# Down projection of a hybrid decoder trunk: weight sums made by accumulating transfers, and eight pairs of k blocks with seven products in place of seven

## The chip, the cores and the metric

The kernel runs on one core of one Trainium2 chip. The metric is the time of one execution on the device in microseconds (us). The kernel before takes 2270.06 us, the median of three runs (2269.26 to 2272.61). The engines of a core work side by side, each through its own queue in order: TensorE (PE, matmuls into PSUM), VectorE (DVE), ScalarE (ACT), GpSimd (POOL) and SyncE (SP), which here only issues transfers.

## The reference

One layer of a decoder: two token mixers, a cross-attention and a feed-forward part, on 256 tokens of 2048 features, float32 throughout. The change touches the last product alone, the down projection of the feed-forward part:

```python
def conv_glu_ffn(u, w_up, conv_w, conv_b, w_down):
    gate, up = jnp.split(u @ w_up, 2, axis=-1)
    gate = causal_dwconv(gate, conv_w, conv_b)
    return (jax.nn.gelu(gate, approximate=False) * up) @ w_down

    # in reference(), for the one layer:
    u = rms_norm(h, ffn_norm_g[l])
    h = h + conv_glu_ffn(u, ffn_w_up[l], ffn_conv_w[l], ffn_conv_b[l], ffn_w_down[l])
    return rms_norm(h, final_norm_g)
```

w_down is 5632 x 2048. The result is added to h and normalised once more.

## The kernel before

**Weights as hi and lo.** Every float32 weight is split into two parts for PE: `hi`, the weight rounded to PE's format (an ACT copy), and `lo`, what is left (a DVE subtraction). The activations are split likewise. A product is then three matmuls, hi x hi, hi x lo and lo x hi (`mm_tok`, 512 columns each).

**The flow of weights.** Weights come in tiles of 128 x 2048 floats (1 MB) in one fixed order (`order`), into three buffers `raw`. `weights()` is called once for every tile that PE is about to use, and issues tiles up to two ahead of it (`AHEAD`): `issue()` starts the transfer on SP, then makes hi and lo in pieces of 1024 columns (L126, L127). hi and lo have five buffers each of 1024 columns (`WB`), which come free as PE has used them. So a `raw` buffer comes free when the tile three before it has been converted, and a conversion waits for its tile's transfer and for a buffer that PE gives back.

**The down projection.** It runs in two halves of 1024 output columns. A half is 22 steps, and a step takes one weight tile: two k blocks of 128 by two column blocks of 512. An ordinary step is 2 x 4 products, 24 matmuls, into four accumulators (2 token blocks x 2 column blocks). A step "with seven products" treats its 2 x 2 blocks in Strassen's way: seven products of sums of blocks in place of eight, 21 matmuls, into the four accumulators and four more (`own`) that collect what several results share. `down_steps` says which steps are of which kind; before, they are steps 2, 5, 8, 11, 14, 17 and 19 of a half, each on a pair q of k blocks, seven pairs in all. Such a step needs

- sums of the four weight blocks, called b11, b22, b12 and b21 (`seven_forms`): four additions on DVE (L164 to L169) in the `raw` tile, in between the conversions (L158, L159), since a sum overwrites a block already converted. It makes seven forms, 3 x 1024 + 512 columns of hi and lo, which take four of the five buffers;
- sums of the four activation blocks (`input_forms`): eight DVE and two ACT instructions for each pair, made once, during the first half (at j = 0, 3, 6, ...), through one buffer `c`, and kept in `xs` and in `ha` for the second half.

**What else stands around.** In each half, `gr` loads the final gain, and at j = 0, 4, 8, 12 `hr` loads two blocks of h, which eight matmuls with the identity add to the accumulators. After the last step with seven products the `own` accumulators are joined into `c` (L1016 to L1023). In the first half that begins with a critical section: ACT loads a function table and copies `own[0]`. The program is cut into blocks there (the UNCONDITIONAL_BRANCH rows below); ACT goes into the section only when everything that the engines and the transfer queues were given in the block before has been done. The other engines do not wait for it. At the very end, for each token block, four results are finished (L1026 add, L1028 square and sum, L1030 gain), a row sum gives the factor r (L1034, L266, L267), and the rows are scaled and stored (L1037 to L1043).

**What sets the order.** A scheduler places the instructions of each engine by its own estimate of when each is ready; the order that a kernel is written in is only its start.

Of the kernel before, what the change touches and what calls it, by code (L numbers as in the profile page):

```python
# [9 lines left out]
F32 = mybir.dt.float32  # L10
# [4 lines left out]
ALU = mybir.AluOpType  # L15
# [4 lines left out]
P = 128  # L20
# [23 lines left out]

NST = 7


def down_steps(half):  # L50
    rest = list(range(NST, KF // 2))
    if half:
        rest = rest[-4:] + rest[:-4]
    steps = []
    for s in range(NST):
        steps += [(False, rest.pop(0)) for _ in range(2 if s < NST - 1 else 1)] + [(True, s)]
    return steps + [(False, k) for k in rest]


# [5 lines left out]
def hybrid_trunk(ctx, tc, xT, memT, par, cst, msk, w_k0, w_ka, w_va, w_hg, w_hv, w_ghg, w_bhg, w_dt,  # L65
# [70 lines left out]
    def issue():  # L136
        seven = state["issued"] in sums
        src, w = fetch()
        cols = w[1]
        nc.sync.dma_start(out=w[0][:, 0:cols], in_=src)  # L140
        if seven:
            ready.append(seven_forms(w[0]))
            return
        half = (cols // 256) * 128
        halves(w, 0, half)
        halves(w, half, cols)
        ready.append(w[2])

    def seven_forms(raw):


        b11, b22, b12, b21 = [raw[:, 512 * i:512 * (i + 1)] for i in range(4)]
        forms = []

        def both(c, d):
            hi = wp.tile([P, 1024], F32R, name="hi", bufs=WB)
            lo = wp.tile([P, 1024], F32R, name="lo", bufs=WB)
            S.copy(out=hi[:, 0:d - c], in_=raw[:, c:d])  # L158
            V.tensor_tensor(out=lo[:, 0:d - c], in0=raw[:, c:d], in1=hi[:, 0:d - c].bitcast(F32),  # L159
                            op=ALU.subtract)  # L160
            forms.extend((hi[:, i:i + 512], lo[:, i:i + 512]) for i in range(0, d - c, 512))

        both(0, 1024)
        V.tensor_tensor(out=b11, in0=b11, in1=b12, op=ALU.add)  # L164
        V.tensor_tensor(out=b12, in0=b12, in1=b22, op=ALU.add)
        V.tensor_tensor(out=b22, in0=b11, in1=b22, op=ALU.add)  # L166
        both(0, 1024)
        both(1024, 2048)
        V.tensor_tensor(out=b21, in0=b22, in1=b21, op=ALU.add)  # L169
        both(1536, 2048)  # L170
        return forms

    background = []

# [750 lines left out]


    fd = ctx.enter_context(tc.tile_pool(name="fd", bufs=1))
    xs = big.tile([P, NST, 3, 256], F32R, name="s2")

    def inputs(k, g):  # L930
# [28 lines left out]
    for i in range(2):  # L959
# [8 lines left out]
        for j, (seven, q) in enumerate(steps):  # L968
            last = i == 1 and j >= len(steps) - 2
            if i == 0:  # L970
                for s in range(NST):
                    if j == 3 * s:
                        input_forms(s)
            w = weights()
            if last and j < len(steps) - 1:
                held = w, q
# [7 lines left out]
            elif seven:  # L984
# [85 lines left out]
def _layout(inp):  # L1070
# [19 lines left out]
    dn = np.stack([np.stack([dn[i, q][[0, 1, 0, 1], [0, 1, 1, 0]] if seven else  # L1090
                             dn[i, q].reshape(4, P, 512) for seven, q in down_steps(i)])
                   for i in range(2)])

# [63 lines left out]
```

## Time and profile before

| | |
|---|---|
| median of three runs | 2270.06 us |
| profiled execution | 2271.94 us, span 2269.6 us |
| PE, DVE, ACT busy | 99%, 71%, 59% |
| GpSimd busy | 1.3 us, nine instructions |
| transfers | 434.81 MB, mean 192 GB/s |
| down projection | about 2018.7 to 2260.4 us of the span on PE, then its tail to 2269.6 |

The view of stretches gives, for each stretch of the span, each engine's busy time with the number of instructions in it, the clock granted to PE, the share of the transfer engines that is busy and the GB/s. A row of the timeline is a start, a duration, an engine, a line, what is written and read, and in brackets the idle time just before it with what ended it. A row of the issues gives the size of a transfer and the time from issue to landing. Rows of groups give busy time, the mean of one in ns, and idle time before with what ended it.

### The profile page before, as it was taken

To read this page: it belongs to the slowest core of one execution; us is meant where nothing else is said; L and a number is where in the kernel's file an instruction comes from. 1 tells how busy PE (TensorE), PEld (TensorE's weight loads), DVE (VectorE), ACT (ScalarE), POOL (GpSimd) and SP (SyncE) were. 2 spreads that over 40 slices of the span, in tenths; PEclk is the share of its full clock that TensorE was granted. 3 is DMA by queue.
4 is the path that set the end of the run, shared out by engine and by line. 5 is a ranking of instruction groups with operands and counts; after the bars stand their busy time and mean duration, and the time that the engine had idled before them with its cause. 6 is when DMAs were issued, how large, how long until landed. Compare 5 with 4: busy or idle time off the path is not lost.

```text
span 2269.6 us, 33643 instructions
## 1 busy us (share of the span) xinstructions
PE 2255.6 (99%) x13368; PEld 1944.1 (86%) x13368; DVE 1622.6 (71%) x2622; ACT 1346.7 (59%) x2028; POOL 1.3 (0%) x9
## 2 busy tenths in 40 slices
PE   9999999999999999999999999999999999999998
PEld 8888888888888888888888888888888888888786
DVE  8878879796446677754576765667777777788776
ACT  7566767676446777854456645556555555555544
POOL 0000000000000000000000000000000000000000
PEclk9999999999999999999999999999999999999999
DMA  8644444546555555455566544565555555555563
GB/s 314 234 171 183 168 170 165 181 154 214 187 198 182 193 186 183 171 181 199 186 237 212 201 167 167 183 217 192 188 186 188 190 194 190 186 204 199 183 230 130
DMA packets 70044, 434.81 MB, mean 192 GB/s; under 512 B 7904, under 2 KB 12544, under 8 KB 20864
## 3 DMA queue, kind: packets, MB, share of 16 engines
q1 hardware_dynamic: 69456, 432.09, 53.7%
q8 instruction: 104, 1.70, 0.3%
q10 hardware_dynamic: 432, 0.58, 0.1%
q14 instruction: 52, 0.43, 0.1%
HBM read 426.32 MB, written 6.32 MB: 191 GB/s over the span
## 4 chain that ended last, share of the span: by engine, by line
PE 98%; DVE 1%; DMA 0%; ACT 0%; issue 0%; SPq 0%; DVEq 0%; ACTq 0%
PE proj L82 88%; PE misc L82 5%; PE lev L82 4%; DVE lo L127 0%; DMA hr<-h_d 0%; PE lev L750 0%; PE lev L686 0%; DMA raw<-in_w_k 0%; DVE e L505 0%; PE lev L830 0%; DVE e L518 0%; DVE lo L159 0%; ACT hi L126 0%; DVE h L1037 0%; DVE sm L564 0%
## 5 line engine op out<-in xcount | busy, mean ns | idle before, releaser
L127 DVE TENSOR_TENSOR lo<-raw,hi 128x1024 fp32r<-128x1024 f32 x738 | 888.5, 1221 | 386.5 <-ACT hi L126 252.5
L126 ACT CAST hi<-raw 128x1024 fp32r<-128x1024 f32 x738 | 771.4, 1049 | 528.3 <-PE proj L82 497.1
L82 PE MATMUL proj<-s,hi 128*128 128x512 f32 x3952 | 953.7, 393 | 0.3 <-ACT hi L343 0.3
L82 PEld LDWEIGHTS proj<-s,hi 128*128 128x128 f32 x3952 | 726.3, 188 | 143.8 <-issue 1.0
L82 PE MATMUL proj<-hi,s 128*128 128x512 f32 x1706 | 534.7, 390 | 0.0
L82 PEld LDWEIGHTS proj<-s,lo 128*128 128x128 f32 x3952 | 509.4, 191 | 20.6
L82 PE MATMUL proj<-s,lo 128*128 128x256 f32 x3952 | 515.9, 283 | 0.0
L82 PEld LDWEIGHTS proj<-hi,s 128*128 128x128 f32 x1706 | 320.1, 188 | 66.3 <-issue 0.3
L82 PE MATMUL proj<-lo,s 128*128 128x512 f32 x853 | 332.1, 389 | 0.0
L82 PEld LDWEIGHTS proj<-lo,s 128*128 128x128 f32 x853 | 160.1, 188 | 32.4
L247 ACT COPY jt<-proj 128x256 f32<-128x256 f32 x199 | 73.4, 369 | 101.5 <-PE proj L82 101.1
L158 ACT CAST hi<-raw 128x1024 fp32r<-128x1024 f32 (+1 forms) x56 | 51.6, 942 | 80.3 <-DVE raw L166 49.2
L909 DVE SCALAR_TENSOR_TENSOR gc<-g,par_t,gc 128x255 f32<-128x255 f32 x88 | 42.6, 484 | 55.1 <-ACT gc L907 53.6
L159 DVE TENSOR_TENSOR lo<-raw,hi 128x1024 fp32r<-128x1024 f32 (+1 forms) x56 | 60.0, 1089 | 26.3 <-ACT hi L158 25.8
L649 DVE SCALAR_TENSOR_TENSOR sz<-t,par_t,sz 128x255 f32<-128x255 f32 (+2 forms) x96 | 46.2, 481 | 20.5 <-ACT sz L646 19.2
L258 DVE SCALAR_TENSOR_TENSOR s<-h,par_t,s 128x256 fp32r<-128x256 f32 x32 | 15.4, 484 | 34.5 <-ACT s L257 34.5
L253 ACT COPY jt<-proj 128x256 f32<-128x256 f32 x32 | 11.8, 371 | 42.2 <-DVE h L252 42.2
L82 PE MATMUL proj<-hi,ha 128*128 128x512 f32 x104 | 36.3, 392 | 0.5 <-ACT hi L158 0.5
L518 DVE TENSOR_TENSOR e<-e,kq 128x256 f32<-128x256 f32 x96 | 34.2, 417 | 0.0
L505 DVE TENSOR_TENSOR e<-bb 128x256 f32<-128x256 f32 x96 | 33.6, 420 | 0.4
L82 PE MATMUL lev<-hi,s 128*128 128x512 f32 x92 | 32.7, 391 | 0.0
L509 ACT ACTIVATE e<-e 128x768 f32<-128x768 f32 x32 | 26.6, 842 | 3.5 <-DVE e L505 3.5
(288 smaller groups left out, 1717.4 us busy)
## 6 DMA issues: line engine op xcount, KB each, us to landing
raw<-in_w_up SPq DMA_DIRECT2D x88, 1024.0 KB, 4.8
raw<-in_w_hg SPq DMA_DIRECT2D x48, 1024.0 KB, 4.8
raw<-in_w_m SPq DMA_DIRECT2D x48, 1024.0 KB, 4.8
raw<-in_w_dn SPq DMA_DIRECT2D x44, 1024.0 KB, 4.8
raw<-in_w_hv SPq DMA_DIRECT2D x16, 1024.0 KB, 4.9
raw<-in_w_ghg SPq DMA_DIRECT2D x16, 1024.0 KB, 4.7
raw<-in_w_bhg SPq DMA_DIRECT2D x16, 1024.0 KB, 4.7
raw<-in_w_gm SPq DMA_DIRECT2D x16, 1024.0 KB, 4.8
```

The lines of the kernel that those rows point to most:

```text
L82: ins = PE.matmul(*args, **kwargs)
L126: S.copy(out=hi[:, c - a:d - a], in_=raw[:, c:d])
L127: V.tensor_tensor(out=lo[:, c - a:d - a], in0=raw[:, c:d], in1=hi[:, c - a:d - a].bitcast(F32), op=ALU.subtract)
L158: S.copy(out=hi[:, 0:d - c], in_=raw[:, c:d])
L159: V.tensor_tensor(out=lo[:, 0:d - c], in0=raw[:, c:d], in1=hi[:, 0:d - c].bitcast(F32), op=ALU.subtract)
L247: S.copy(out=tmp, in_=ps[:, T:2 * T])
L258: V.scalar_tensor_tensor(out=dst[:, T:2 * T], in0=src, scalar=g, in1=dst[:, 0:T].bitcast(F32), op0=ALU.mult, op1=ALU.subtract)
L505: V.tensor_tensor(out=lev[hw].rearrange("p (n c i) -> p n c i", c=2, i=hw), in0=free(bb, 0, [(2 * hw, nb), (T + hw, 2), (1, hw)]), in1=fre ...
L509: S.activation(out=e[j], in_=e[j], func=AF.Exp)
L518: V.tensor_tensor(out=ev, in0=ev, in1=free(kq, 0, [(2 * hw, nb), (T + hw, 2), (1, hw)]), op=ALU.mult)
L649: V.scalar_tensor_tensor(out=o[:, s:T], in0=raw[:, 0:T - s], scalar=pc("m2_cw", 4 * c + 3 - s), in1=o[:, s:T], op0=ALU.mult, op1=ALU.add)
L909: V.scalar_tensor_tensor(out=gc[:, s:T], in0=g[:, 0:T - s], scalar=pc("f_cw", 3 * c + 2 - s), in1=gc[:, s:T], op0=ALU.mult, op1=ALU.add)
```

## The change

Three things change.

*Two of the four weight sums are made by transfers.* The tile of a step with seven products now comes in parts. SP loads three blocks and a second copy of the first of them into `raw`, and b11 into a tile of its own (one buffer, `b11`). GpSimd then issues two transfers that add a block from memory to what lies in `raw`: these give the sums t1 and t3. DVE makes the other two (L173, L175 of the changed kernel). Conversions (L166, L167) are 512 + 3 x 1024 columns as before. Such a tile now moves 1.79 MB instead of 1.05 MB.

*Eight pairs instead of seven.* The steps with seven products are now 2, 5, 8, 10, 13, 15, 17 and 19 of a half. Input forms are made at every second step instead of every third, eight times.

*The seven products come in another order:* own[0], own[1], acc[1], acc[0], own[3], own[2], acc[2], which is the order in which the forms are now made.

```diff
-NST = 7
+NST = 8
...
-    for s in range(NST):
-        steps += [(False, rest.pop(0)) for _ in range(2 if s < NST - 1 else 1)] + [(True, s)]
+    for s, ordinary in enumerate((2, 2, 2, 1, 2, 1, 1, 1)):
+        steps += [(False, rest.pop(0)) for _ in range(ordinary)] + [(True, s)]
...
+        if seven:
+            ready.append(seven_forms(src, w[0]))
+            return
         nc.sync.dma_start(out=w[0][:, 0:cols], in_=src)
-        if seven:
-            ready.append(seven_forms(w[0]))
-            return
...
-        b11, b22, b12, b21 = [raw[:, 512 * i:512 * (i + 1)] for i in range(4)]
...
+        b11 = extra[0].tile([P, 512], F32, name="b11")
+        nc.sync.dma_start(out=raw[:, 0:1536], in_=src[:, 0:1536])
+        nc.sync.dma_start(out=raw[:, 1536:2048], in_=src[:, 0:512])
+        nc.sync.dma_start(out=b11, in_=src[:, 1536:2048])
+        G.dma_start(out=raw[:, 0:512], in_=src[:, 1536:2048], accum_op=ALU.add)
+        G.dma_start(out=raw[:, 1536:2048], in_=src[:, 512:1024], accum_op=ALU.add)
...
-        both(0, 1024)
-        V.tensor_tensor(out=b11, in0=b11, in1=b12, op=ALU.add)
-        V.tensor_tensor(out=b12, in0=b12, in1=b22, op=ALU.add)
-        V.tensor_tensor(out=b22, in0=b11, in1=b22, op=ALU.add)
-        both(0, 1024)
-        both(1024, 2048)
-        V.tensor_tensor(out=b21, in0=b22, in1=b21, op=ALU.add)
-        both(1536, 2048)
-        return forms
+        b11, = both(b11)
+        t1, b22 = both(raw[:, 0:1024])
+        V.tensor_tensor(out=raw[:, 512:1024], in0=raw[:, 0:512], in1=raw[:, 512:1024], op=ALU.add)
+        b21, t3 = both(raw[:, 1024:2048])
+        V.tensor_tensor(out=raw[:, 1024:1536], in0=raw[:, 512:1024], in1=raw[:, 1024:1536], op=ALU.add)
+        t2, t4 = both(raw[:, 512:1536])
+        return [b11, b22, t1, t2, t3, b21, t4]
...
-                for s in range(NST):
-                    if j == 3 * s:
-                        input_forms(s)
+                if j % 2 == 0 and j < 2 * NST:
+                    input_forms(j // 2)
...
                 mm_tok(own[0], a11, w[0], **one)
+                mm_tok(own[1], y1, w[2], **one)
                 mm_tok(acc[1], x4, w[1])
-                mm_tok(own[1], y1, w[2], **one)
+                mm_tok(acc[0], a12, w[5])
+                mm_tok(own[3], y3, w[4], **one)
                 mm_tok(own[2], x2, w[3], **one)
-                mm_tok(own[3], y3, w[4], **one)
-                mm_tok(acc[0], a12, w[5])
                 mm_tok(acc[2], a22, w[6])
```

`both` now makes the hi and lo of one part and returns them in pieces of 512 columns. `_layout` stores the blocks of such a tile in the order that these transfers read.

The scheduler places things anew. Three places matter below. In the rows, numbers behind a name tell buffers apart; a line number of the changed kernel is some six higher than that of the same line before.

ACT at the switch between the halves, before: raw_20033 is the tile of step 19, raw_20086 that of step 20, and lev_19308 is own[0].

```order
L158 CAST hi_20042<-raw_20033 128x1024
L158 CAST hi_20046<-raw_20033 128x1024
L1015 NO_OP
L1153 UNCONDITIONAL_BRANCH
L1016 ACT_TABLE_LOAD
L1017 COPY c_20151<-lev_19308 128x512
L1015 UNCONDITIONAL_BRANCH
L1015 NO_OP
L158 CAST hi_20051<-raw_20033 128x512
L126 CAST hi_20088<-raw_20086 128x1024
```

And now, where raw_20083, raw_20129 and raw_20163 are the tiles of steps 19, 20 and 21:

```order
L166 CAST hi_20099<-raw_20083 128x1024
L166 CAST hi_20104<-raw_20083 128x1024
L126 CAST hi_20131<-raw_20129 128x1024
L126 CAST hi_20135<-raw_20129 128x1024
L1021 NO_OP
L1159 UNCONDITIONAL_BRANCH
L1022 ACT_TABLE_LOAD
L1023 COPY c_20194<-lev_19308 128x512
L1021 UNCONDITIONAL_BRANCH
L126 CAST hi_20165<-raw_20163 128x1024
```

The last conversion of step 19 and both of step 20 moved from behind the table load to ahead of it.

SP at the same place, now (raw_20203 is the tile of the second half's first step, which stood behind the branch before):

```order
L143 DMA raw_20129<-in_w_dn 128x2048
L143 DMA raw_20163<-in_w_dn 128x2048
L158 DMA b11_20294<-in_w_dn 128x512
L143 DMA raw_20203<-in_w_dn 128x2048
L1159 UNCONDITIONAL_BRANCH
L143 DMA raw_20237<-in_w_dn 128x2048
```

One more tile is issued ahead of the block's end, and so stands among what ACT's section waits for.

DVE at the end of the program, before:

```order
L1034 TENSOR_REDUCE r<-ss 128x1
L1026 TENSOR_TENSOR h<-misc,h 128x512 x2
L1037 TENSOR_SCALAR h<-h,r 128x512
L1042 TENSOR_SCALAR c<-c,r 128x1024
L1030 TENSOR_TENSOR h<-h,gr 128x512 x2
L1034 TENSOR_REDUCE r<-ss 128x1
```

And now:

```order
L1040 TENSOR_REDUCE r<-ss 128x1
L1032 TENSOR_TENSOR h<-misc,h 128x512
L1036 TENSOR_TENSOR h<-h,gr 128x512
L1043 TENSOR_SCALAR h<-h,r 128x512
L1048 TENSOR_SCALAR c<-c,r 128x1024
L1032 TENSOR_TENSOR h<-misc,h 128x512
L1036 TENSOR_TENSOR h<-h,gr 128x512
L1040 TENSOR_REDUCE r<-ss 128x1
```

The last add and the last product by the gain moved behind the scaling of the other token block, and the first of the two products ahead of it.

DVE at the start of the down projection, now; L917, L938 and L942 of before are L923, L945 and L949, and the tile raw_19324 is that of step 2:

```order
L923 TENSOR_TENSOR gc_19242<-gc_19242,up_19291 128x256
L269 TENSOR_TENSOR h_14717<-gc_19242,h_14717 128x256
L945 TENSOR_TENSOR c_19314<-ha_14716 128x2x256
...
L945 TENSOR_TENSOR c_19503<-ha_14716 128x2x256
L167 TENSOR_TENSOR lo_19332<-b11_19325,hi_19331 128x512
L949 TENSOR_TENSOR c_19503<-c_19503 128x128
L167 TENSOR_TENSOR lo_19336<-raw_19324,hi_19335 128x1024
L167 TENSOR_TENSOR lo_19341<-raw_19324,hi_19340 128x1024
L173 TENSOR_TENSOR raw_19324<-raw_19324 128x512
```

Before, the first conversions and sums of step 2 stood between the last instructions of the up projection; now two whole input forms and the start of a third stand ahead of them.

More of the change, by code (lines that the diff above doesn't have):

```diff
@@ L147, in issue, with seven_forms, both @@
         ready.append(w[2])
-    def seven_forms(raw):
-        b11, b22, b12, b21 = [raw[:, 512 * i:512 * (i + 1)] for i in range(4)]
-        forms = []
-        def both(c, d):
+    extra = []
+    def seven_forms(src, raw):
+        b11 = extra[0].tile([P, 512], F32, name="b11")
[4 more added lines that the diff above has]
+        G.dma_start(out=raw[:, 1536:2048], in_=src[:, 512:1024], accum_op=ALU.add)
+        def both(part):
+            cols = part.shape[-1]
             hi = wp.tile([P, 1024], F32R, name="hi", bufs=WB)
             lo = wp.tile([P, 1024], F32R, name="lo", bufs=WB)
-            S.copy(out=hi[:, 0:d - c], in_=raw[:, c:d])
-            V.tensor_tensor(out=lo[:, 0:d - c], in0=raw[:, c:d], in1=hi[:, 0:d - c].bitcast(F32),
+            S.copy(out=hi[:, 0:cols], in_=part)
+            V.tensor_tensor(out=lo[:, 0:cols], in0=part, in1=hi[:, 0:cols].bitcast(F32),
                             op=ALU.subtract)
-            forms.extend((hi[:, i:i + 512], lo[:, i:i + 512]) for i in range(0, d - c, 512))
-        both(0, 1024)
-        V.tensor_tensor(out=b11, in0=b11, in1=b12, op=ALU.add)
-        V.tensor_tensor(out=b12, in0=b12, in1=b22, op=ALU.add)
-        V.tensor_tensor(out=b22, in0=b11, in1=b22, op=ALU.add)
-        both(0, 1024)
-        both(1024, 2048)
-        V.tensor_tensor(out=b21, in0=b22, in1=b21, op=ALU.add)
-        both(1536, 2048)
-        return forms
+            return [(hi[:, i:i + 512], lo[:, i:i + 512]) for i in range(0, cols, 512)]
+        b11, = both(b11)
[5 more added lines that the diff above has]
+        return [b11, b22, t1, t2, t3, b21, t4]
     background = []
@@ L927, in hybrid_trunk @@
     fd = ctx.enter_context(tc.tile_pool(name="fd", bufs=1))
+    extra.append(fd)
     xs = big.tile([P, NST, 3, 256], F32R, name="s2")
@@ L1089, in _layout @@
     dn = inp["ffn_w_down"][0].reshape(KF // 2, 2, P, 2, 2, 512).transpose(3, 0, 1, 4, 2, 5)
-    dn = np.stack([np.stack([dn[i, q][[0, 1, 0, 1], [0, 1, 1, 0]] if seven else
+    dn = np.stack([np.stack([dn[i, q][[0, 1, 1, 0], [1, 1, 0, 0]] if seven else
                              dn[i, q].reshape(4, P, 512) for seven, q in down_steps(i)])
```

## The prediction

> **What bounds the kernel now.** I read the page's busy times and chain of waits first, then the transfer issues, then the down projection in stretches of 5 us, then the stretches that stood out.
>
> ```profile
> PE 2255.6 (99%) x13368; PEld 1944.1 (86%) x13368; DVE 1622.6 (71%) x2622; ACT 1346.7 (59%) x2028; POOL 1.3 (0%) x9
> PE 98%; DVE 1%; DMA 0%; ACT 0%; issue 0%; SPq 0%; DVEq 0%; ACTq 0%
> raw<-in_w_dn SPq DMA_DIRECT2D x44, 1024.0 KB, 4.8
> h<-in_xT SPq DMA_DIRECT2D x4, 512.0 KB, 12.3
> hr<-h_d SPq DMA_DIRECT2D x8, 256.0 KB, 4.6
> out<-h SPq DMA_DIRECT2D x2, 256.0 KB, 2.3
> ```
>
> TensorE (PE) is the bound: 99% busy, 98% of the chain, 2269.6 - 2255.6 = 14 us idle in the span. GpSimd (POOL) does nothing and issues no transfer. An edit helps by removing matmuls, by closing one of those gaps, or at the tail.
>
> ```profile
> 2040.00:2045.00 5.00, 5.00 (x23) 4.14 (x23) 4.93 (x9) 2.12 (x3) 0.00 (x0) 1.00 0.37 154
> 2120.00:2125.00 5.00, 5.00 (x24) 4.14 (x23) 3.05 (x3) 2.45 (x3) 0.00 (x0) 1.00 0.01 2
> 2125.00:2130.00 5.00, 3.78 (x14) 2.21 (x13) 2.90 (x3) 4.73 (x7) 0.00 (x0) 0.92 0.28 74
> 2130.00:2135.00 5.00, 5.00 (x18) 3.97 (x17) 4.96 (x7) 2.64 (x3) 0.00 (x0) 0.74 1.00 411
> 2260.00:2265.00 5.00, 0.44 (x2) 0.02 (x1) 3.92 (x8) 2.34 (x6) 0.00 (x0) 1.00 0.54 210
> 2115.49 6.80 PE proj L82 x30
> ```
>
> The columns after the stretch are busy PE, weight load, DVE, ACT, POOL, then granted clock, DMA share and GB/s. Full stretches hold 24 matmul records; the chain's row gives 6.80/30 = 0.227 us a matmul. Three things matter. At 2040 VectorE (DVE) is nearly full, 4.93 of 5, though PE never waits for it there. At 2125 to 2135, the switch between the halves of the projection, PE gets 14 and 18 records instead of 24, at clocks 0.92 and 0.74: 16 matmuls x 0.227 = 3.6 us lost. From 2260.4 on PE is done and a tail runs.
>
> **The change part by part.**
>
> *Fewer products.* Two more steps take seven products: 2 x 3 = 6 matmuls fewer, -6 x 0.227 = **-1.36 us**.
>
> *The switch.* Why PE stalls there:
>
> ```profile
> 2126.86 0.50 PE L82 MATMUL proj<-hi,ha 128*128 128x512 f32 x1 [0.49 <-ACT hi L158]
> 2129.07 0.68 PE L82 MATMUL proj<-lo,h 128*128 128x512 f32 x1 [0.51 <-DVE lo L127]
> 2122.97 0.69 DVE L169 TENSOR_TENSOR raw<-raw 128x512 f32<-128x512 f32 x1
> 2124.05 1.28 ACT L1016 ACT_TABLE_LOAD   x1 [2.55 <-DVE raw L169]
> 2125.34 0.59 ACT L1017 COPY c<-lev 128x512 f32<-128x512 f32 x1
> 2126.19 0.62 ACT L158 CAST hi<-raw 128x512 fp32r<-128x512 f32 x1 [0.26 <-ACTq L1015]
> ```
>
> ScalarE (ACT) loads its table after everything that the first block issued, here DVE's last sum, ending 2123.66. Behind the load and the copy stands the last hi of step 19, and behind that those of steps 20 and 21. PE waits, three times in short order, and then the clock drops. In the new order ACT converts all of step 19 and both halves of step 20 ahead of the load. What it newly waits for is the transfer of raw_20203 (the second half's first step), which now stands ahead of the block's end on SP and needs step 19's last conversion. With t0 the PE start of step 19: that conversion's last buffer comes free 12 matmuls into step 18, t0 - 2.7; hi and lo (1.05 and 1.22 below) end at t0 - 0.4; landing 4.8 later is t0 + 4.4; the load and copy (1.28 + 0.59, and about 0.5 of handing over, as from 2123.66 to 2124.05) end near t0 + 6.9; step 21's first hi is ready at t0 + 7.9. PE needs it after 21 + 24 matmuls, t0 + 10.2. So 2.3 us are spare, and the whole loss goes: **-3.6 us**. If that cover is gone the wait is step 21's.
>
> *The tail.*
>
> ```profile
> 2260.48 0.69 DVE L1026 TENSOR_TENSOR h<-misc,h 128x512 f32<-128x512 f32 x1 [1.69 <-PE misc L82]
> 2261.09 0.48 DVE L1037 TENSOR_SCALAR h<-h,r 128x512 f32<-128x512 f32 x1
> 2261.48 0.75 DVE L1042 TENSOR_SCALAR c<-c,r 128x1024 f32<-128x1024 f32 x1
> 2262.14 1.29 DVE L1030 TENSOR_TENSOR h<-h,gr 128x512 f32<-128x512 f32 x2
> 2263.35 0.15 DVE L1034 TENSOR_REDUCE r<-ss 128x1 f32<-128x4 f32 x1
> 2259.46 0.19 ACT L267 ACTIVATE r<-r 128x1 f32<-128x1 f32 x1
> 2261.74 0.19 ACT L1028 ACTIVATION_READ_ACCUMULATOR misc<-h 128x1 f32 x1
> ```
>
> The reduce needs ACT's sum, there at 2261.93, and stands behind four other DVE instructions until 2263.35. In the new order one gain product and the two scalings stand before the last add. r is there at 2259.65, so scalings run 2259.65 to about 2260.8; the add starts 2260.8 instead of 2260.48, ACT's sum is there at 2262.25, one product (0.65) fits in between, and the reduce starts at about 2262.3: **-1.1 us**, since all that follows hangs on it.
>
> *The first steps.*
>
> ```profile
> 2022.32 0.33 SPq L967 DMA_DIRECT2D gr<-in_fin_g  x1
> 2026.80 1.13 PE L82 MATMUL proj<-cst_t,hr 128*128 128x128 f32 x8 [0.20 <-DMA hr<-h_d]
> 2027.68 0.48 PE L82 MATMUL proj<-hi,ha 128*128 128x512 f32 x1
> 2030.99 0.39 PE L82 MATMUL lev<-hi,ha 128*128 128x512 f32 x1
> 2020.89 0.42 DVE L917 TENSOR_TENSOR gc<-gc,up 128x256 f32<-128x256 f32 x1
> 2022.76 0.69 DVE L938 TENSOR_TENSOR c<-ha 128x512 f32<-128x512 f32 x1
> 2023.97 1.02 DVE L942 TENSOR_TENSOR c<-c 128x128 f32<-128x128 f32 x4
> 2026.37 0.55 DVE L945 TENSOR_TENSOR s<-c,s 128x384 fp32r<-128x384 f32 x1
> 2026.84 0.28 DVE L948 TENSOR_TENSOR ha<-c,ha 128x128 fp32r<-128x128 f32 x1
> L127 DVE TENSOR_TENSOR lo<-raw,hi 128x1024 fp32r<-128x1024 f32 x59 | 71.4, 1223 | 17.3 <-ACT hi L126 13.1 <-PE proj L82 1.1
> L158 ACT CAST hi<-raw 128x1024 fp32r<-128x1024 f32 x42 | 42.9, 1049 | 52.4 <-DVE raw L166 49.2 <-DMA raw<-in_w_dn 1.4 <-ACT proj L1028 0.6
> L159 DVE TENSOR_TENSOR lo<-raw,hi 128x512 fp32r<-128x512 f32 x14 | 9.7, 691 | 11.1 <-ACT hi L158 11.1
> L166 DVE TENSOR_TENSOR raw<-raw 128x512 f32<-128x512 f32 x14 | 9.7, 690 | 0.4
> ```
>
> The old first weight sums stood among the last up-projection work on DVE; now L917 comes 1.13 us sooner (an lo of 1.22 no longer ahead of it), and gr's issue, which waits for that work, too. b11 goes in between, one issue of 0.33. hr is thus about 0.8 us earlier and PE reaches it three matmuls later: the 0.20 wait goes, **-0.2 us**. The b11 of the first seven-step lands near 2021.4 + 4.6 = 2026. DVE is then still on input forms: from 2021.0 two of 0.69 + 1.02 + 0.28 + 0.55 = 2.5, about 0.3 each for ACT's casts in between, and the first add of a third, to 2027.2. Then come two lo, 0.69 and 1.22, another lo of 1.22, two sums of 0.69 and two form instructions of 0.28, some 5 us with overlaps taken off, to 2031.8 or so, and a last hi and lo, 1.05 and 1.22, to 2034.1. PE started that step at 2030.99, now 2030.8, and needs the last lo after 16 matmuls, 2034.4. It just fits, with no lead left.
>
> *DVE and ACT.* A seven-step cost DVE 3 x 1.22 + 0.69 + 4 x 0.69 = 7.1 us and costs 3 x 1.22 + 0.69 + 2 x 0.69 = 5.7, against 21 x 0.227 = 4.8 on PE. The eighth input form and the closer spacing of forms take back most of that in the first half. Off PE's path either way: 0.
>
> *The accumulating transfers.* No row shows a transfer issued by GpSimd or one that adds. Call A the time from the plain landing to the added data. Below it is 2.3 us (a plain 256 KB store); above 12.3, the page's longest, in a crowded queue; I take 4.6, the 256 KB load into SBUF of the same stretch, nearest in size and direction. What it must fit: a seven-step's raw buffer is one of three, so in the spacing seven, two ordinary, seven, it comes from the seven-step before. That loop is landing 4.8 + A + a conversion chain of hi 1.05, lo 1.22, sum 0.69, lo 1.22, sum 0.69, hi 1.05, lo 1.22 = 7.1, so 11.9 + A. PE takes 21 + 48 matmuls, 15.7 us, and about 0.9 more (2026.80 to 2027.68) in the loops with eight hr matmuls. At A = 4.6 the loop is 16.5: level. At 2.3 nothing is lost; with input forms cutting in I allow **+0.5 us**. There are three such loops a half (steps 2, 5, 8 and 10, 13). Level is near A = 5, so I reckon a loss of 3 x (A - 5) in the first half, which starts with no lead, and in the second as much less 4 us, the lead of a last conversion there (t0 - 0.4 above) over PE's need of it (16 matmuls into the step).
>
> The Trainium skill (DMA: Bandwidth & Descriptors, Anatomy of one DMA) fits a GpSimd-issued transfer as 2.0 us plus bytes over 436 GB/s. For 256 KB that is an estimate of 2.6 us, near the lower end; the sum by it would be without the 0.5. No run here shows it, and the page's fit is not for adding ones.
>
> *Sum.* -1.36 - 3.6 - 1.1 - 0.2 + 0.5 = -5.8 us. The profiled execution took 2271.94 (span 2269.6 and 2.3 around it), 1.9 above the median of the runs, 2270.06; I take the difference over to the median: **2264.3 us**.
>
> **Rivals.**
>
> *Adds too late (slower).* The loop above outgrows PE. The gains, 6.3 us, are used up where 3 x (A - 5) + 3 x (A - 5) - 4 = 6.3, at A = 6.7; at A = 8 the stalls are 14 us: 2270.06 - 6.3 + 14 = 2277.8. For it: GpSimd's issue is in no row, and each add must also read its destination. Against: of the eight hr loads of this size the median is 4.6.
>
> *Adds somewhat late.* A of 6 costs 3 us in the first half, where DVE has no room to catch up (4.93 of 5), and nothing in the second: 2270.06 - 6.3 + 3 = 2266.8; at 6.5 it is 4.5 + 0.5: 2268.8. No change.
>
> *The switch keeps its loss.* If raw_20203 lands over 2.3 us later than reckoned, ACT's table load is late for step 21 and the clock drops again: 2264.3 + 3.6 = 2268. For it: ACT now waits for a transfer that it did not wait for. Against: the spare time.
>
> *DVE holds GpSimd up.* If GpSimd could build its transfers only between DVE's instructions, each of two adds would wait up to 1.22 us: A = 4.6 + 2.4 = 7.0, 6 + 2 = 8 us of stalls: 2271.8, no change. No row bears on it. The Trainium skill (SBUF — State Buffer, Who interferes with whom) says that a DVE instruction with two SBUF inputs holds up a GpSimd instruction that reads SBUF, but infers that building transfers, which writes, is free of it.
>
> **How the numbers follow.** My forecast 0.50, with its own range 2262.5 to 2266; somewhat late 0.13; the switch 0.12; DVE holding up 0.05; adds too late 0.17; 0.03 for a gain beyond the forecast. The range 2262.5 to 2273 leaves out most of the slower case and little below. A measurement of this kernel tells 0.2%, 4.5 us, from no change, so faster is below 2265.5: most of my forecast (0.46) and 0.03. Same is 0.34: the rest of the forecast and the three middle rivals. Slower 0.17.
>
> **What would show it.** Matmuls: 6 fewer. Switch: full stretches around the table load, clock 1.00, the load waiting for a transfer. Tail: reduce about 1.8 us after PE's last matmul instead of 2.9. Adds: issue to landing on a POOL queue near 4.6 us. Wrong: PE waits for hi or lo of a seven-step, above all in its first three, with those waiting for the added transfer; or the clock below 1 in the first half.

## The result, and the profile after

The changed kernel takes **2307.14 us**, the kernel before beside it 2271.34 us: a ratio of 1.0163 (95% interval 1.0151 to 1.0175), 36 us slower. That is above the predicted range, where a gain had been forecast. The profiled execution took 2307.46 us, its span 2305.5.

First the page of the changed kernel: busy times, the chain of waits by engine and by line, the queue of GpSimd's transfers (packets, MB, share of the time of 16 engines), the busiest conversion (busy, mean ns, idle before and what ended it), and the transfer issues (size, median time to landing).

```profile
PE 2266.9 (98%) x13362; PEld 1943.3 (84%) x13362; DVE 1610.7 (70%) x2609; ACT 1351.0 (59%) x2034; POOL 29.5 (1%) x41
PE 87%; DVE 5%; DMA 5%; issue 1%; ACT 1%; ACTq 0%; POOL 0%; DVEq 0%; SPq 0%; POOLq 0%
q0 software_dynamic: 4608, 8.39, 2.1%
L166 ACT CAST hi<-raw 128x1024 fp32r<-128x1024 f32 x48 | 49.9, 1050 | 125.5 <-DMA raw<-in_w_dn 68.2
raw<-in_w_dn POOLq DMA_DIRECT2D x32, 256.0 KB, 7.8
raw<-in_w_dn SPq DMA_DIRECT2D x28, 1024.0 KB, 5.6
b<-in_w_dn SPq DMA_DIRECT2D x16, 256.0 KB, 7.5
```

Six matmuls are gone, as counted. But the chain, 98% PE before, now has 5% DVE and 5% transfers, and ACT stood idle 125.5 us before the conversions of the steps with seven products (L166; "seven-steps" from here on). The adding transfers landed a median 7.8 us after their issue, not 4.6, and the plain tiles beside them, 4.8 before, take 5.6.

How much PE lost is read from its first and last matmul of the projection: 241.7 us before and 277.5 now. At 0.2267 us a matmul, and 0.11 for each of the 64 with the identity, the work is 236.9 and 235.6 us. What is over, PE's waits and the matmuls slowed by a lower clock behind them, I call stalls: **4.8 us before and 41.9 now**. By steps, the large ones now are those of steps 5, 8, 13 and 17 of each half, all with seven products: 7.0, 4.2, 3.3, 4.5 and 4.1, 5.0, 1.7, 5.1 us. The 37.1 more of stalls, 1.36 less for the six matmuls, a start 0.4 later and a tail 0.3 shorter make the 35.9 by which the spans differ.

Step 5 of the first half shows how a stall comes about. Three timelines of the changed kernel, of PE, ACT and GpSimd (start, duration, instruction, idle time before it and what ended it):

```profile
2051.06 0.50 PE L82 MATMUL lev<-hi,s 128*128 128x512 f32 x1 [1.20 <-ACT hi L166]
2052.32 0.50 PE L82 MATMUL lev<-lo,s 128*128 128x512 f32 x1 [0.76 <-DVE lo L167]
2057.13 0.50 PE L82 MATMUL misc<-hi,s 128*128 128x512 f32 x1 [1.41 <-ACT hi L166]
...
2039.20 0.30 ACT L954 CAST ha<-c 128x128 fp32r<-128x128 f32 x1
2049.96 1.05 ACT L166 CAST hi<-raw 128x1024 fp32r<-128x1024 f32 x1 [10.47 <-PE lev L82]
2051.94 1.05 ACT L166 CAST hi<-raw 128x1024 fp32r<-128x1024 f32 x1 [0.93 <-DMA raw<-in_w_dn]
2056.98 3.89 ACT L126 CAST hi<-raw 128x1024 fp32r<-128x1024 f32 x4
...
2041.01 0.86 POOL L159 DMA_DIRECT2D raw<-in_w_dn  x1 [25.53 <-DVE lo L167]
2041.55 1.22 POOL L160 DMA_DIRECT2D raw<-in_w_dn  x1
```

GpSimd issues the adds at 2041.0 and 2041.6, as the blocks land. ACT, done at 2039.5, stands idle 10.5 us until the first sum is there at 2049.8 (the bracket names PE, but it is not PE that holds this conversion: in the kernel without adds below it starts at 2041.0), and the second add lands at 2051.8. So the added data come **10.7 us** after the plain landing (2041.1): this is the prediction's A. The tiles of steps 6 and 7 lie in their buffers from 2045.9 and 2049.6 on, but ACT converts them only after the seven-step, at 2056.98. The same stretch in the view of stretches (busy PE, weight load, DVE, ACT, POOL, then clock, share of the transfer engines, GB/s):

```profile
2040.00:2045.00 5.00, 5.00 (x24) 4.14 (x23) 3.31 (x9) 0.00 (x0) 1.76 (x2) 1.00 0.94 307
2045.00:2050.00 5.00, 4.86 (x26) 3.84 (x24) 0.00 (x0) 0.04 (x1) 0.00 (x0) 1.00 0.97 263
2050.00:2055.00 5.00, 2.86 (x10) 1.85 (x11) 3.21 (x4) 2.67 (x4) 0.00 (x0) 1.00 0.22 61
2055.00:2060.00 5.00, 2.84 (x9) 1.76 (x8) 4.93 (x8) 3.97 (x5) 0.00 (x0) 0.82 0.15 21
```

The transfer engines are full for ten microseconds and then nearly idle. DVE and ACT, which did 4.93 and 2.12 us of work in the first of these stretches before, do next to nothing for five us and have it all to do at the end, while PE waits and loses clock (0.82) as well.

### The profile page after: what moved, and what is told of

It is laid out like the page before. It is cut to its first block, busy times and chain, and to the rows that moved or that the text cites. A ratio compares the mean times of both kernels' runs of the same rounds, so it can differ in the third digit from the quotient of the medians.

```text
span 2305.5 us, 33818 instructions
## 1 busy us (share of the span) xinstructions
PE 2266.9 (98%) x13362; PEld 1943.3 (84%) x13362; DVE 1610.7 (70%) x2609; ACT 1351.0 (59%) x2034; POOL 29.5 (1%) x41
## 3 DMA queue, kind: packets, MB, share of 16 engines
q0 software_dynamic: 4608, 8.39, 2.1%
## 4 chain that ended last, share of the span: by engine, by line
PE 87%; DVE 5%; DMA 5%; issue 1%; ACT 1%; ACTq 0%; POOL 0%; DVEq 0%; SPq 0%; POOLq 0%
PE proj L82 82%; DMA raw<-in_w_dn 4%; PE misc L82 3%; PE lev L82 2%; DVE lo L127 2%; DVE lo L167 1%; ACT hi L166 1%; DVE raw L175 0%; DMA b<-in_w_dn 0%; PE lev L692 0%; PE lev L756 0%; DMA par_t<-in_par 0%; DVE raw L173 0%; DVE c L949 0%; POOL raw L159 0%
## 5 line engine op out<-in xcount | busy, mean ns | idle before, releaser
L127 DVE TENSOR_TENSOR lo<-raw,hi 128x1024 fp32r<-128x1024 f32 x734 | 881.8, 1221 | 378.1 <-ACT hi L126 248.5
L126 ACT CAST hi<-raw 128x1024 fp32r<-128x1024 f32 x734 | 766.7, 1051 | 505.8 <-PE proj L82 488.5
L166 ACT CAST hi<-raw 128x1024 fp32r<-128x1024 f32 x48 | 49.9, 1050 | 125.5 <-DMA raw<-in_w_dn 68.2
L167 DVE TENSOR_TENSOR lo<-raw,hi 128x1024 fp32r<-128x1024 f32 x48 | 58.6, 1223 | 81.7 <-ACT hi L166 81.5
L159 POOL DMA_DIRECT2D raw<-in_w_dn x16 | 14.0, 874 | 2132.4 <-DMA raw<-in_w_dn 1979.5
L259 ACT COPY jt<-proj 128x256 f32<-128x256 f32 x32 | 11.9, 373 | 42.1 <-DVE h L258 42.1
```

Source lines behind the costliest of these rows:

```text
L126: S.copy(out=hi[:, c - a:d - a], in_=raw[:, c:d])
L127: V.tensor_tensor(out=lo[:, c - a:d - a], in0=raw[:, c:d], in1=hi[:, c - a:d - a].bitcast(F32), op=ALU.subtract)
L159: G.dma_start(out=raw[:, 0:512], in_=src[:, 1536:2048], accum_op=ALU.add)
L166: S.copy(out=hi[:, 0:cols], in_=part)
L167: V.tensor_tensor(out=lo[:, 0:cols], in0=part, in1=hi[:, 0:cols].bitcast(F32), op=ALU.subtract)
```

## The experiments

My theory after the result: the adding transfers alone make the loss, since the time A from the plain landing to the added data is 10 us and not 4.6, so that the loop through a raw buffer outlasts PE. Rivals: the eighth pair and the closer spacing; GpSimd's issue; the load that the adds put on the other transfers. "Stalls" below is worked out as above, and each ratio is to the kernel before timed in the same session.

| kernel | us | ratio to before, 95% interval | stalls, us |
|---|---|---|---|
| eight pairs, DVE sums, old order | 2272.42 | 1.0007, 0.9998 to 1.0016 | 6.7 |
| seven pairs, adds, new order | 2319.17 | 1.0216, 1.0202 to 1.0230 | 55.2 |
| the change without its adds | 2266.90 | 0.9983, 0.9974 to 0.9992 | 1.7 |
| copies in place of adds | 2288.32 | 1.0076, 1.0061 to 1.0092 | 24.4 |
| the change with DVE sums | 2267.62 | 0.9984, 0.9975 to 0.9993 | 2.9 |
| one add of two | 2290.34 | 1.0088, 1.0072 to 1.0103 | 22.7 |
| five pairs, wider apart | 2293.98 | 1.0095, 1.0082 to 1.0109 | 23.6 |
| plain tiles in 2 KB pieces | 2310.30 | 1.0173, 1.0159 to 1.0187 | 44.4 |
| seven pairs, adds apart | 2309.66 | 1.0166, 1.0151 to 1.0181 | 43.8 |
| eight pairs, adds apart | 2323.53 | 1.0226, 1.0211 to 1.0241 | 56.4 |
| half of the plain bytes | 2293.51 | 1.0096, 1.0079 to 1.0113 | 28.5 |
| adds that nobody waits for | 2267.38 | 0.9987, 0.9978 to 0.9997 | 2.4 |

**Which part of the change: pairs or adds.** Three kernels. The first takes the old `seven_forms` and the old order of products into the changed kernel; the second takes the old number and pattern of steps; the third only drops the adds.

```diff
 (first, against the change)
+        both(0, 1024)
+        V.tensor_tensor(out=b11, in0=b11, in1=b12, op=ALU.add)
 ... (seven_forms and the seven products as before)
 (second, against the change)
-NST = 8
+NST = 7
 (third, against the change)
-        G.dma_start(out=raw[:, 0:512], in_=src[:, 1536:2048], accum_op=ALU.add)
-        G.dma_start(out=raw[:, 1536:2048], in_=src[:, 512:1024], accum_op=ALU.add)
```

> Eight pairs with seven products, in the new pattern of steps and with input forms every two steps, but all four weight sums on DVE and the products in the old order. Theory (the two adding transfers make the loss: their data come 10 us after the plain landing, not 4.6): no transfer on GpSimd's queue, no new stalls in the seven-steps; 1.36 us less for six matmuls, the stall at the switch between the halves stays at 3.7, DVE has up to 2 us of delays: 2268 to 2273. Rival (the eighth pair and the closer spacing do it: three raw buffers don't allow seven, one ordinary, seven): PE loses 2 us and more in steps 10, 13, 15, 17, 19 of each half also without the transfers: 2280 to 2300.

> Seven pairs in the old pattern and with the old spacing of input forms, but two of the four sums by adding transfers and the products in the new order. Theory (the adding transfers): the loop from one seven-step to the next is 22 us against 16.6 on PE, so 3 to 5 us are lost in each of five steps a half, 30 to 45 in all, against 2 to 3 gained at the switch: 2297 to 2312, PE waiting for hi and lo of the steps 5, 8, 11, 14, 17. Rival (eighth pair and closer spacing): 2266 to 2272, since only the switch and the order change.

> The changed kernel without its two adding transfers of a seven-step; the sums t1 and t3 are thereby left out and everything else, the order of the plain transfers, of conversions and products, is the same. Theory (the adds): all stalls above 1 us but those of step 1 and the switch go, so this is what the change would give if its adds took no time and no bandwidth: 2263 to 2269. Rival (closer spacing): still over 2285. Rival (the four plain pieces of a seven-step, 1.25 MB for 1 MB, are what crowds the transfers): 2275 to 2290, with plain landings of 7 us or more.

Eight pairs with all sums on DVE cost nothing that can be told from before (2272.42); seven pairs with adds are slower still than the change (2319.17, above the 2312 that I allowed); the change without adds is 4 us faster than before. The spacing is not it: the adds are, and the room that the rest of the change leaves is 2266.9. The three plain pieces (768, 256 and 256 KB), which stay in the third kernel, cost nothing on PE beyond 1.3 us in step 1. The eighth pair in the old order gains nothing either: its six matmuls (1.36) go into 1.9 us more of stalls. The switch still takes 3.0 of them (steps 17 to 20, 3.7 before), and steps 18 to 20 of the second half (1.8) and step 11 of the first (0.7) are new.

**Adding, or being a transfer of GpSimd.** The same two transfers as plain copies, with the same waiters:

```diff
-        G.dma_start(out=raw[:, 0:512], in_=src[:, 1536:2048], accum_op=ALU.add)
-        G.dma_start(out=raw[:, 1536:2048], in_=src[:, 512:1024], accum_op=ALU.add)
+        G.dma_start(out=raw[:, 0:512], in_=src[:, 1536:2048])
+        G.dma_start(out=raw[:, 1536:2048], in_=src[:, 512:1024])
```

> The changed kernel with the two transfers of GpSimd made plain copies of the same 256 KB to the same place, behind the same landings and with the same waiters; the sums t1 and t3 are left out. If the adding itself is slow (the destination read, added and written): issue to landing falls to 4 to 5 us and more than half of the 36 us goes, 2270 to 2288. If it is where and when these transfers run (issued by GpSimd, behind a plain landing, beside the next plain 1 MB): landing stays at 7 to 9 us and the time at 2300 to 2310.

Of the 40.2 us that the change lies above the kernel without adds (2307.14 - 2266.9), 18.8 go; 2288.32 is 0.3 above the first outcome's range and far below the second's. Landing falls, but only to a median of 5.2 and 6.8 us. First the two adds of the change, then the two copies and the copies' queue; the copies' landing is 2.9 us at best and the adds' 3.7:

```profile
DMA to landing us min/median/max: 3.7/7.4/8.8
DMA to landing us min/median/max: 3.8/9.1/10.5
```

```profile
DMA to landing us min/median/max: 2.9/5.2/7.1
DMA to landing us min/median/max: 3.0/6.8/8.3
q0 software_dynamic: 2560, 8.39, 1.1%
2040.00:2045.00 5.00, 5.00 (x23) 4.14 (x23) 3.70 (x9) 0.57 (x2) 1.06 (x2) 1.00 1.04 417
```

The queue rows price it. 32 adds took 4608 packets, 144 each, and 2.1% of 16 engines' 2305.5 us: 24.2 us of one engine each, 1.5 us of all sixteen. 32 copies of the same bytes took 80 packets each and 1.1% of 2287.1: 12.6 us, 0.8 of all. An add costs the transfer engines **1.9 times** a copy. With copies they moved 417 GB/s when full, with adds 263. So in time about half of the loss is the adding, and half is one more transfer between the landing and the conversion. That transfer was always one of GpSimd's; a copy issued by SP in its place wasn't tried.

The Trainium skill (Collectives: The Full Stack, The bandwidth ceiling: the fold count and why AG ≠ RS ≠ AR) says of a reducing transfer in a collective that it reads two sources with two descriptors for each piece, and so reaches half of a copy's rate, 1.93 times slower in its measurement. The rows here agree for an add within one core: 1.9 times the time, and 144 packets against 80.

**One add instead of two.**

```diff
-        G.dma_start(out=raw[:, 0:512], in_=src[:, 1536:2048], accum_op=ALU.add)
+        V.tensor_tensor(out=raw[:, 0:512], in0=raw[:, 0:512], in1=b, op=ALU.add)
 ... (b is the tile of b11)
```

> The changed kernel with one adding transfer a seven-step (t3); t1 is made by DVE. Theory (the loop through a raw buffer holds the time from the plain landing to the last added data, and the two adds share the transfer engines with each other and with plain tiles): the added data come 6 to 8 us after the plain landing instead of 10, and t3 is needed one conversion later than t1, so over half of the 40 us goes: 2278 to 2290. Rival (the wait for any transfer of GpSimd is what costs, one or two alike): 2298 to 2308.

2290.34, 0.3 above the range of the theory, and 7.7 below the rival's. Its one add lands after a median of 4.9 us (8.2 at most).

**The loop of buffers.** Five pairs, on steps 3, 7, 11, 15, 19:

```diff
-NST = 8
+NST = 5
...
-    for s, ordinary in enumerate((2, 2, 2, 1, 2, 1, 1, 1)):
+    for s, ordinary in enumerate((3, 3, 3, 3, 3)):
 ... (input forms every four steps)
```

> The changed kernel with five pairs instead of eight, on steps 3, 7, 11, 15, 19 of a half: three ordinary tiles between two seven-steps, so that a seven-step's raw buffer comes from an ordinary tile and not from the seven-step before; 18 matmuls more, 4.1 us. Both adding transfers stay. Theory (the loop seven-step to seven-step through three buffers): the adds are as slow as before, 7 to 10 us, but have one more tile's time: 0 to 1.5 us lost in each of ten, 2271 to 2285. Rival (each seven-step loses its 4 us wherever it stands, for the capacity of the transfer engines or for the conversions alone): 2300 to 2315.

Between the two ranges. The adds are as late as in the change (second add 9.4 us, median), and the stalls inside the ten seven-steps fall to 12.4 us, 1.2 each against 2.3 in the change. But 4.1 of 18 matmuls more, 5.1 in step 1 (PE waits there for hr, which comes beside two adds and takes 7.0 us) and 5.7 around the switch and after the last seven-step are lost in other places. A wider loop helps, and doesn't hide an A of 10.

**What makes the adds late.** Two things could: turns between transfers by pieces (8 KB for a plain tile, 2 KB for an add), or the sum of the work in flight. The first kernel issues plain tiles in pieces of 512 columns; the second halves their bytes.

```diff
 (first)
-        nc.sync.dma_start(out=w[0][:, 0:cols], in_=src)
+            for c in range(0, cols, 512):
+                nc.sync.dma_start(out=w[0][:, c:c + 512], in_=src[:, c:c + 512])
 (second)
+        nc.sync.dma_start(out=w[0][:, 0:cols // 2], in_=src[:, 0:cols // 2])
 ... (both only in the down projection; the second converts the loaded half twice)
```

> The changed kernel with the plain tiles of ordinary steps issued as four transfers of 512 columns, so that their pieces for a partition are 2 KB like those of the adds and not 8 KB. Theory of the share (the engines take turns between queues by pieces, so that 8 KB pieces leave the 2 KB adds little): the adds' issue to landing falls from 8 to 5 or 6 us and the stalls by a third or more: 2280 to 2297. Rival (the adds are slow by their own cost in the engines and by the sum of bytes): landing stays at 7 to 10, 2303 to 2315, since SP also has three more issues of about 0.4 a tile.

> The changed kernel with the ordinary tiles of the down projection loaded by half (1024 of 2048 columns, which stand for both halves in the conversions; the other half of these weights is left out). The adds, their issue and their bytes are the same. Theory (shared time): two plain tiles beside the adds take half of their 2.9 us each of all sixteen engines, so the added data come about 7 us after the plain landing, not 10: 2275 to 2290. Rival (the adds' own time or GpSimd's issue): as the change, 2300 to 2308.

Smaller pieces don't help: 2310.3, the adds' landing 6.9 and 9.0. Fewer bytes do: 5.9 and 7.2, and 13.6 us of time, though 2293.51 is above the theory's range. What counts is the sum of the work: around step 5 the engines are busy for 0.94 x 5 + 0.97 x 5 + 1.1 (0.22 of the next 5) = 10.7 us with the last of a tile, two plain tiles, b11 and two adds, and the second add lands when all of that is done. (A tile of a seven-step moves seven blocks of 0.262 MB, 1.84 MB, not the 1.79 given with the change.) The changed kernel has the other case too: in steps 10, 15 and 19 of each half no 1 MB tile is in flight when the adds are issued, the second add lands after 3.8 to 6.2 us, and A is 4.1 to 6.8. In steps 2, 5, 8, 13 and 17 the second add takes 8.0 to 10.5 us, and A is 9.0 to 11.0.

**Adds apart from plain tiles.** GpSimd writes 64 elements of the second sum into the next tile's buffer, so its load waits; on seven pairs and on eight. `behind` holds the buffer of the last seven-step.

```diff
+        if behind:
+            G.tensor_copy(out=w[0][0:1, 0:64], in_=behind.pop()[0:1, 1536:1600])
         nc.sync.dma_start(out=w[0][:, 0:cols], in_=src)
```

> The kernel of the seven-pair experiment with adds (2319), in which the plain tile behind a seven-step, and all that stands behind it on SP, is held until that step's second add has landed (GpSimd writes 64 elements of the add's result into the tile's buffer, which the load then overwrites). So the adds run with nearly nothing beside them. Theory (the adds are late because all transfers in flight share the engines' time, and they have two 1 MB tiles beside them): issue to landing falls from 9 to about 4, the added data come 5 us after the plain landing, and most of the 55 us of stalls goes although the plain tiles come later: 2268 to 2282. Rival (an add takes this long on its own, or GpSimd's issue does): landing stays at 7 or more, and the plain tiles come late in addition: 2315 or more.

> The changed kernel with the same hold. Theory (shared time): adds land 4 us after issue and the long stalls of steps 5 and 8 go; where a seven-step follows after one ordinary tile its own tile is held too, and a chain of adds, tile, adds of about 13 us for two steps stands against 10.2 on PE, so up to 3 us are lost in some of the steps 10, 15, 17, 19: 2272 to 2295. Rival (adds slow on their own): 2307 or more.

The adds do land sooner: on seven pairs a median of 4.3 and 5.9 us where they took 8.1 and 9.5, on eight 4.0 and 5.4. But neither time is in the theory's range: 2309.66 lies between the two ranges, and 2323.53 in the rival's. Two stretches of the seven-pair kernel in which only adds and one b11 are moved, and two of its waits:

```profile
2064.50:2066.50 2.00, 2.00 (x6) 1.63 (x5) 2.00 (x5) 0.00 (x0) 0.16 (x1) 0.50 1.03 165
2066.50:2068.50 2.00, 2.00 (x9) 1.59 (x9) 0.56 (x3) 1.39 (x3) 0.00 (x0) 0.94 0.95 206
ACT hi L169 <- DMA raw<-in_w_dn: 69.7, 19, 9.3
ACT hi L126 <- DMA raw<-in_w_dn: 22.9, 12, 5.1
```

Even alone the two adds fill the engines, at 165 GB/s (206 with b11 beside them), and the second lands 5.4 us after its issue (2063.45 to 2068.86), A = 5.9. Where they ran like this the loop from one seven-step's transfer to the next was 17.3 and 16.8 us (2058.24 to 2075.53, 2093.60 to 2110.36), close to PE's 16.6; in the change it was 22.5 (2035.84 to 2058.36). Yet the time fell by 9.5 us on seven pairs, not by the 37 or more that I expected, and on eight it rose by 16.

Two things are seen. The last row is the first: ordinary conversions (L126) now wait 22.9 us for their tiles, where without the hold they waited for none, so part of the lateness went from the adds to the tiles held behind them. In the first half the seven-steps 8, 11, 14 and 17 have no stall, and the ordinary steps 12, 15 and 18 have 1.9, 1.5 and 4.4 us. The other is that the hold missed tiles: in steps 5, 11 and 14 of each half SP had put another plain tile ahead of the held one, and the second add took 5.7 to 9.5 us. So the seven-steps' own conversions (L169) still wait 69.7 us, and those of the second half still stall. On eight pairs 13.8 us are lost in step 19 alone, 6.8 of them because the table load at the switch waited for a tile that SP issued behind a held one. A hold that catches every tile wasn't tried.

**The wait, or the load.** That left open whether PE suffers from its own conversions' wait or from the load on the engines. The last kernel keeps both adds and their moment, but into the gain's buffer:

```diff
+        one, two = gr[-1][:, 0:512], gr[-1][:, 512:1024]
+        G.tensor_copy(out=one[0:1, 0:64], in_=raw[0:1, 0:64])
+        G.dma_start(out=one, in_=src[:, 1536:2048], accum_op=ALU.add)
 ... (the second add likewise, behind raw[0:1, 1536:1600])
```

> The changed kernel with its two adds of 256 KB issued at the same moment (a copy of 64 elements on GpSimd makes each follow the plain landing), but into the gain's buffer gr, where no conversion waits for them; so t1 and t3 are left out and the gain is spoilt. The engines of the transfers carry the same load as in the change. It splits the 40 us that the change lies above the kernel without adds (2266.9). If it is the wait of the seven-step's own conversions for the adds: the plain tiles land at 6 to 9 us in place of 4.8 but have a tile's time to spare, and the time is 2267 to 2274. If it is that the adds hold up the plain tiles: 2285 or more, with PE waiting for hi and lo of ordinary tiles too. In between: both.

2267.38, no more than without adds, and 39.8 us below the change. Issues, queue and the stretch of step 5 in this kernel:

```profile
q0 software_dynamic: 4608, 8.39, 2.2%
raw<-in_w_dn SPq DMA_DIRECT2D x28, 1024.0 KB, 5.9
gr<-in_w_dn POOLq DMA_DIRECT2D x32, 256.0 KB, 8.0
2045.00:2050.00 5.00, 5.00 (x28) 4.28 (x27) 4.38 (x10) 2.71 (x4) 0.00 (x0) 1.00 1.04 276
```

Adds as late as in the change, plain tiles slower than in it (5.9 for 5.6), engines as full (1.04, 276 GB/s), and PE doesn't lose a matmul in it. So the load on the transfers costs nothing by itself here, where each plain tile has a tile's time to spare; the wait for hr in the wide kernel's step 1 shows the other case. **The loss, 39.8 of its 40.2 us, is that the seven-step's conversions wait for the added data**, and that ACT and DVE, in order, hold everything else behind them.

**A kernel that beats both.** The new order of forms and products with t1 and t3 on DVE:

```diff
-        G.dma_start(out=raw[:, 0:512], in_=src[:, 1536:2048], accum_op=ALU.add)
-        G.dma_start(out=raw[:, 1536:2048], in_=src[:, 512:1024], accum_op=ALU.add)
+        V.tensor_tensor(out=raw[:, 1536:2048], in0=raw[:, 0:512], in1=raw[:, 512:1024], op=ALU.add)
+        V.tensor_tensor(out=raw[:, 0:512], in0=raw[:, 0:512], in1=b, op=ALU.add)
 ... (the second copy of the first block isn't loaded)
```

> The changed kernel with its order of forms and products, but t1 and t3 made by DVE in the place where the transfers added them; the tile comes as three blocks and b11, 1 MB in all. Theory (only the adding transfers cost): the switch keeps what it gained (stall about 0 to 1.4 in place of 3.7), six matmuls fewer, two sums of 0.69 more on DVE a seven-step than with transfers: 2266 to 2270, no seven-step with a stall over 1 us. Rival (DVE is too full for four sums at this spacing, so something had to leave it): stalls of 1 to 2 us in the steps 10, 13, 15, 17, 19: 2274 to 2285.

2267.62 us, 0.16% faster than before (interval 0.07 to 0.25%), as the theory said. Against the first kernel of this section, which has the same pairs and as many sums on DVE, the order of forms and products (with the tile in two pieces) is worth 4.8 us. Stretches and ACT's table load at the switch, and step 5:

```profile
2040.00:2045.00 5.00, 5.00 (x24) 4.14 (x23) 4.97 (x8) 1.69 (x4) 0.00 (x0) 1.00 1.00 375
2130.00:2135.00 5.00, 5.00 (x24) 4.09 (x23) 1.82 (x2) 4.77 (x6) 0.00 (x0) 1.00 0.39 162
2130.04 1.28 ACT L1022 ACT_TABLE_LOAD   x1 [3.61 <-DMA raw<-in_w_dn]
```

DVE is as full as it was (4.97 of 5) and PE waits for nothing there: four sums a step on DVE were never a cost.

## Why the prediction was wrong

**The step that failed** is the price of A: "I take 4.6, the 256 KB load into SBUF of the same stretch, nearest in size and direction". It measured 10.7 in step 5 of the first half and 10.1 and 10.0 in its steps 8 and 13 (2063.26 to 2073.36, 2095.08 to 2105.12), 9.0 to 11.0 in ten of the sixteen seven-steps. Near 4.6 it came only in steps 10 and 15, 4.1 to 5.1. The row was a wrong neighbour in two ways. It is a copy, and an add takes the engines 1.9 times a copy's time. And its median hid what was beside such a load: of the eight hr loads before, the four issued right behind a plain tile took 5.2 to 5.8 us, the other four 2.7 to 4.0. The adds of step 5 are issued when two plain tiles have just been: what then matters is the work in flight. That could have been summed from rows of before: a plain tile takes 1.05 MB / 411 GB/s = 2.6 us of full engines, two of them 5.1, and adds that also read what they add to, as the rival's "for it" said, 1.3 each: 7.7, and b11, which is more than the break-even of 6.7. The lower end, 2.3, was no bound at all: the least that an add took in any kernel here is 3.5. The room was mis-sized a little too: 16.6 of PE less 11.9 leaves 4.7, not 5, so even at 4.6 the loop had nothing to spare.

**The loss formula** gave the right sign and too little. With A = 10 it is 15 + 11 = 26 us, a time of 2289.8; the large stalls were 34.9. It counted three loops a half, and the trace has four stalls a half (steps 5, 8, 13, 17): step 17's tile comes into the buffer of step 14's, which ACT converts behind the late ones of step 13 (from 2109.3, step 13's last at 2108.4), and so is issued at 2113.0; its A was 10.4 once more. The last run of the experiments shows that the plain tiles, though slower, took no part.

**Adds too late (slower)**, with 0.17, is what happened, by its own mechanism and place, with its break-even; only its A of 8 was too small. The milder rival, somewhat late with an A of 6 to 6.5, was passed as well. Its chance was too small because the one row against it, the median of 4.6, mixed loads with and without a tile beside them.

**DVE holds GpSimd up**: not so. In 2045 to 2050 DVE did nothing (0.00) while both adds were under way and landed after 8.8 and 10.3 us; with DVE full (2.00 of 2.00 in the stretch from 2064.5 of the seven-pair kernel with adds apart) an add landed after 3.8, and DVE was full at its issue (2062.9) as well. What GpSimd itself spent on an issue is 0.86 and 1.22 us, with DVE busy or not. The Trainium skill's fit that I had named (DMA: Bandwidth & Descriptors, Anatomy of one DMA), an estimate of 2.6 us for 256 KB, is near the best plain copy here, 2.9, and below every add, 3.5 at the least.

**The switch.** The mechanism was right and the sum, where tiles come in time, too: the load waits for raw_20203's transfer and the stretches around it are full (24 records, clock 1.00, in the kernel with DVE sums above). In the change a part was lost again, by the rival's way. The changed kernel's ACT, and PE's last wait there:

```profile
2149.68 1.28 ACT L1022 ACT_TABLE_LOAD   x1 [4.39 <-DMA raw<-in_w_dn]
2150.97 0.59 ACT L1023 COPY c<-lev 128x512 f32<-128x512 f32 x1
2154.10 0.49 PE L82 MATMUL proj<-lo,h 128*128 128x512 f32 x1 [0.76 <-DVE lo L127]
```

1.4 us of stalls remain of 3.7.

**The tail** gave 0.3 us, not 1.1. The step "one product (0.65) fits in between, and the reduce starts at about 2262.3" overlooked that the product writes the tile that ACT's square reads, and so waits for it:

```profile
2297.05 0.69 DVE L1032 TENSOR_TENSOR h<-misc,h 128x512 f32<-128x512 f32 x1
2298.53 0.69 DVE L1036 TENSOR_TENSOR h<-h,gr 128x512 f32<-128x512 f32 x1 [0.79 <-ACT misc L1034]
2299.14 0.15 DVE L1040 TENSOR_REDUCE r<-ss 128x1 f32<-128x4 f32 x1
```

The reduce starts 2.6 us after PE's last matmul (2296.58), not 1.8.

**The first steps** lost 1.0 us instead of gaining 0.2: step 1 stalls 1.5 us where it stalled 0.5. gr, b11 and hr are now all in flight with the tile issued before them; hr took 6.1 us and b11 5.9, for which I had 4.6, and the scheduler put the first product of step 2 ahead of the identity matmuls, so that PE stood until b11 was converted. The kernels without adds keep this stall (1.3 to 1.7).

**Fewer products**: right, 1.36 us. **DVE and ACT at nothing**: right; the kernels with DVE sums and without adds lie 0.7 us apart, less than their intervals.

## What to carry to other kernels

A transfer that is put between a load and its first use is priced by the work in flight when it is issued, not by the landing of a quiet row, and an adding one by twice its bytes. Before moving work off an engine, see whether anyone waits for that engine: DVE was full and nobody did, so the sums taken from it bought nothing, and their new place had a wait of 10 us in a loop that had none to spare. To tell a wait from a load, let the same transfer run where nobody waits for it.

## What the runs showed of the hardware

An adding transfer of 256 KB takes 144 packets and 24.2 us of engine time (the changed kernel), a copy issued in the same way 80 and 12.6 (copies in place of adds). At best an add lands 3.5 us after its issue, a copy 2.9. Two adds with nothing beside them keep all sixteen engines busy at 165 GB/s (seven pairs, adds apart), so a full share says little of the bytes moved. With two 1 MB tiles beside them they land after 8.8 and 10.3 us (step 5 of the change), with these tiles in pieces of 2 KB after 8.3 and 9.8, and the tiles after 7.8 and 9.2 in place of 4.8; yet where nobody waited for the adds, PE lost nothing by them.
